# Transposes in one-chunk steps, a group's last banks emptied at once, seven products in K pairs 4 and 5, and a rough scale of the input, in an fp32 decoder layer

## The chip, the cores and the metric

One core of a Trainium2 chip runs the whole layer as one launch. The metric is the device time of that launch in microseconds: the median of several runs.

## What is computed

A decoder layer on 256 rows of width 2048, in fp32 (cut from the reference; the attention and the convolution are described below, since the change doesn't touch them):

```python
def swiglu(h, w_gate, w_up, w_down):
    return (jax.nn.silu(h @ w_gate) * (h @ w_up)) @ w_down

x = x + 0.5 * swiglu(rms_norm(x, ffn1_norm[l]), ffn1_w_gate[l], ffn1_w_up[l], ffn1_w_down[l])
x = x + hybrid_mixer(rms_norm(x, mix_norm[l]), w_in[l], b_gate[l], conv_w[l], ...)
x = x + 0.5 * swiglu(rms_norm(x, ffn2_norm[l]), ffn2_w_gate[l], ffn2_w_up[l], ffn2_w_down[l])
return rms_norm(x, final_norm)
```

The inner width of the two FFNs is 5632. `hybrid_mixer` is a combined projection into q, k, v, three convolution inputs and two gates, attention over 16 heads of 128, a short convolution, and three projections back.

## The kernel before, in words

**Products.** Every fp32 operand is kept as two parts: `hi`, rounded to the fp32r type, and `lo`, the rest. A product of a tile of 128x128 activations with 128x512 weights is three matmul pieces: hi by hi, hi by lo, lo by hi (L230 to L232). The weights come in tiles of 128x1024 fp32 (512 KB, called a chunk here: two K tiles of 512 columns), by SP's DMA queue (L793) into five buffers `w`. ScalarE makes `hi` (L824), VectorE `lo` = w - hi (L825). Four buffers each of `hi` and `lo` stand ready, so the split of a chunk waits until TensorE has finished the chunk four before it.

**Groups.** An FFN is a list of groups (`group`): gate and up groups over 1024 columns each (`gu`), and down groups (`down`). A group sums over 8 pairs of K tiles (16 tiles of 128 rows of the weights) into four PSUM banks `C[i, n]` (i: rows 0 to 127 or 128 to 255; n: left or right 512 columns). A plain pair is two chunks of 12 pieces. In a pair of the list `FAST` a seven-product scheme is used for the 2x2 block product: instead of 8 products 7, with sums of weight tiles, which VectorE makes (L797, four additions of 128x512 in `usum`), and sums of activation tiles, made when these are turned (`sums`). Such a pair has four chunks, of 6, 3, 6 and 6 pieces ("a", "b", "s1", "s2"), and its own four banks M[1], M[5], M[6], M[7], three of them (psS, psT, psV) those in which transposes are made too. Thirteen groups of each FFN have fast pairs; before they are pairs 1 and 3 (counted from 0).

**Order.** One program order is recorded by hand: `advance` puts the splits of chunks up to four ahead on ScalarE and VectorE, then TensorE's pieces of the chunk are recorded, then `flush(1)` records one piece of pending work: an entry of `pending` (emptying of banks), or else one of `turns` (transposes). While `banks_held`, from the first fast pair until all M banks are emptied, no turn is recorded. An engine runs its instructions in that order.

**Emptying.** `drain(C, n)` empties the two banks of n: after a gate group L497 combines them with the M sums and L471 applies silu into `gbuf`; after an up group L497 and L477 or L475 multiply `gbuf`. n = 0 is emptied in place; n = 1 is an entry of `pending`, recorded behind the next group's first chunk (`Step(chunks, pe, [lambda: drain(C, 1)])`).

**Turning.** The product of gate and up in `gbuf` is turned by transposes on TensorE (L309), two K tiles to a call of `turn_pair`, and split into `ring`. All of a `turn_pair` is recorded at once: transposes, copies (L102, L103, L315), sums (L296 to L301). The input of an FFN is turned in the same way (`turn_x`) into `xn`. For the second FFN its rows are scaled first by a rough scale, from the first quarter of the columns (L396, within the same call); the exact scale over the rough one is applied later. For the first FFN the exact scale of all of x is computed at the start, x is scaled (L878, L879) into `sacc`, and turned.

Of the kernel before, what the change touches and what calls it, by code (L numbers as in the profile page):

```python
# [14 lines left out]
P = 128  # L15
# [13 lines left out]
WARM = 11  # L29
FAST = (1, 3)  # L30
RING = 16
# [20 lines left out]
def macaron_kernel(ctx: ExitStack, tc: tile.TileContext, xt, gf, cst, wg1, wu1, wd1, win, wv, wao,  # L52
# [38 lines left out]

    work.tile([P, LINE + 112], F32, name="padw", tag="padw", bufs=1)

# [33 lines left out]
    def norm_cols(tag, i0=0, i1=2, blocks=NB):  # L127

        n = i1 - i0
        r = work.tile([P, 8], F32, name="rc", tag="rc", bufs=4)  # L130
# [82 lines left out]
    def group(wa, wb, k0, pairs, src, fast, xsum, early, drain):  # L213
# [77 lines left out]
    def sums(slot, a1, a2):  # L291
# [6 lines left out]
        nc.vector.tensor_add(x3, a2[:, 0:P], x6)  # L298
        nc.vector.tensor_sub(x7, a1[:, 0:P], a1[:, P:T])
        nc.scalar.copy(at[:, slot, :], c4)  # L300
        nc.vector.tensor_sub(at[:, slot + 1, :], c4, f32(at[:, slot, :]))  # L301

    def turn_pair(src, dst, gain, slot):

        keep = []
        for q, tag in ((0, "psT"), (1, "psV")):
            ps = patt.tile([P, 4 * P], F32, name=tag, tag=tag)
            for i in range(2):
                nc.tensor.transpose(ps[:, i * P:(i + 1) * P], src(q, i), ident)  # L309
            if slot is None:  # L310
                split_col(dst(q), ps[:, 0:T], None if gain is None else gain(q))
            else:
                a = tmp("a")
                if gain is None:
                    nc.scalar.copy(a, ps[:, 0:T])  # L315
                else:
                    nc.scalar.activation(a, ps[:, 0:T], AF.Copy, scale=gain(q))
                split_col(dst(q), a)
                keep.append(a)
        if keep:  # L320
            sums(slot, *keep)

    def turn_x(m, src, goff):

        slot = X_SUMS + 2 * FAST.index(m // 2) if m // 2 in FAST else None
        turn_pair(lambda q, i: src(m + q, i), lambda q: xn[:, m + q, :], lambda q: vec(goff, m + q), slot)

# [26 lines left out]

    def turn(m, gain):

# [6 lines left out]
    def residual(nb, factor, tag, gain):  # L363
# [16 lines left out]
        if tag == "f2":  # L380
            def done(pv):
                add(pv)
                if nb == 0:
                    scale0[0] = norm_cols(tag, blocks=1)
                if nb == NB - 1:
                    r = norm_cols(tag)
                    q = work.tile([P, 8], F32, name="rc", tag="rc", bufs=4)
                    nc.vector.reciprocal(q[:, 0:2], scale0[0])
                    nc.vector.tensor_mul(q[:, 2:4], r, q[:, 0:2])
                    rcol[tag] = q[:, 2:4]  # L390

                def scaled(m, i):
                    if i == 0:
                        t = pair[m] = tmp("xs")
                        for j in range(2):
                            nc.vector.tensor_scalar(t[:, j * P:(j + 1) * P], x[:, j, m * P:(m + 1) * P],  # L396
                                                    scale0[0][:, j:j + 1], None, op0=ALU.mult)
                    return pair[m][:, i * P:(i + 1) * P]
                pair = {}
                for m in (4 * nb, 4 * nb + 2):  # L400
                    turns.append(lambda m=m: turn_x(m, scaled, gain))
            return [done]
        if tag is None or tag == "fin":
            return [add]
        return [add, lambda _: None] + [lambda _, m=m: turn(m, gain) for m in range(4 * nb, 4 * nb + 4)]

# [11 lines left out]

    scale0 = [None]
    grow = {}  # L420
# [36 lines left out]

    def ffn(tag, wg, wu, wd, gain_next, next_tag, first=False):
        sign = {(0, 0): (0, ALU.add), (0, 1): (2, ALU.subtract), (1, 0): (3, ALU.add), (1, 1): (1, ALU.subtract)}
# [9 lines left out]
        def gate(i, src, cols):  # L469
            s = 1.0 if first else rcol[tag][:, i:i + 1]  # L470
            nc.scalar.activation(gbuf[:, i, cols], src, AF.Silu, scale=s)  # L471

        def up(i, src, cols):
            if first:
                nc.vector.tensor_mul(gbuf[:, i, cols], src, gbuf[:, i, cols])  # L475
            else:
                nc.vector.scalar_tensor_tensor(gbuf[:, i, cols], src, rcol[tag][:, i:i + 1], gbuf[:, i, cols],  # L477
                                               op0=ALU.mult, op1=ALU.mult)

        def hidden(q, t):  # L480

            k0 = next(a for a, b in ROUNDS if a <= t < b)
            p = (t - k0) // 2
            slot = H_SUMS + 2 * FAST.index(p) if p in FAST and k0 != ROUNDS[-1][0] else None
            turn_pair(lambda e, i: gbuf[:, i, (2 * q + e) * P:(2 * q + e + 1) * P],
                      lambda e: ring((t + e) % RING), None, slot)

        def gu(which, b):
            fast = () if (which, b) == ("g", 0) else FAST
            use = gate if which == "g" else up  # L490

            def drain(C, n):
                for i in range(2):
                    src = C[i, n]
# [4 lines left out]
                    use(i, src, slice(n * NW, (n + 1) * NW))  # L499
                if which == "u" and n == 1:  # L500
                    for q in range(4):
                        turns.append(lambda q=q: hidden(q, 8 * b + 2 * q))
            w = wg if which == "g" else wu
# [3 lines left out]
        def gu_last(n_block):  # L507
            def drain(C, n):
                for i in range(2):
                    (gate, up)[n](i, C[i, n], slice(0, NW))  # L510
                if n == 1:
                    for q in range(2):
                        turns.append(lambda q=q: hidden(q, 4 * n_block + 2 * q))
            steps.append(group(wg[n_block], wu[n_block], 0, ND // 2, lambda k: xn[:, k, :], (), None, None, drain))
# [256 lines left out]

    ffn("f1", wg1, wu1, wd1, GM, "mix", first=True)
    mixer(G2, "f2")
# [80 lines left out]
    nc.scalar.preload_act_table(AF.Sqrt)  # L854
    nc.sync.dma_start(cs[:, 0:NCST], cst)
    for nb in range(NB):
        cols = slice(nb * NW, (nb + 1) * NW)
        nc.sync.dma_start(x[:, :, cols], xt[:, :, cols])
    load(4)
    nc.vector.memset(gbuf[:, 0, 0:T], 0.0)  # L860
    warm = patt.tile([P, 4 * P], F32, name="psS", tag="psS")
    for _ in range(WARM):
        nc.tensor.matmul(warm[:, 0:T], gbuf[:, 0, 0:P], gbuf[:, 0, 0:T], start=True, stop=True)
    make_identity(nc, ident)
    for q0, sl in ((0, slice(0, P)), (P, slice(P, 3 * P))):
# [4 lines left out]
                                fill=NEG, base=q0, channel_multiplier=1)  # L870
    for nb in range(NB):
        for i in range(2):
            row_square("f1", i, nb, at[:, 8 + i, :])
    r = norm_cols("f1")
    cut(1)
    for nb in range(NB):
        cols = slice(nb * NW, (nb + 1) * NW)
        nc.vector.tensor_scalar(yout[:, 0, cols], x[:, 0, cols], r[:, 0:1], None, op0=ALU.mult)  # L878
        nc.scalar.activation(yout[:, 1, cols], x[:, 1, cols], AF.Copy, scale=r[:, 1:2])  # L879
    turns = []  # L880
    scaled_in = lambda m, i: yout[:, i, m * P:(m + 1) * P]
    for m in range(0, ND, 2):
        turns.append(lambda m=m: turn_x(m, scaled_in, G1))
    turns.pop(0)()
    turns.pop(0)()

    done = 0

    holding = False
    pending = []  # L890

# [6 lines left out]
    def flush(n=None):  # L898
        while pending and not holding and n != 0:
            pending.pop(0)()  # L900
            n = None if n is None else n - 1
        while turns and not banks_held and n != 0:
            turns.pop(0)()
            n = None if n is None else n - 1

# [68 lines left out]
```

## Time and profile before

| | us |
|---|---|
| median of 3 runs | 2530.03 |
| lowest and highest | 2527.68, 2531.37 |
| the profiled execution | 2531.69 |
| its span, first to last instruction | 2529.6 |
| TensorE busy | 2471.9 |
| VectorE busy | 1773.1 |
| ScalarE busy | 1231.9 |

A busy time is the union of an engine's instructions; the pieces of TensorE overlap one another in the rows, so their rate is read from start to start. The granted clock of TensorE over the span is 0.989: short stretches run at 0.5 (1.2 GHz), the rest at full rate (2.4 GHz). The program holds 11955 matmul instructions before and after.

### The profile page before, as it was taken

How to read it: one execution, taken by the hardware profiler on the slowest of the kernel's cores; microseconds unless marked ns; L12 is line 12 of the kernel's file. 1: busy time of each engine (PE TensorE's matmuls, PEld its weight loads, DVE VectorE, ACT ScalarE, POOL GpSimd, SP SyncE). 2: the span in 40 equal slices, each digit the busy share in tenths (PEclk: the TensorE clock that was granted, in tenths of full speed). 3: DMA queues.
4: the chain of work that ended last, by engine and by line, in shares of the span. 5: the costliest groups of instructions: out<-in, count | busy, mean ns of one | idle time of the engine just before them, and what ended most of it. 6: DMA issues, size and time to landing. Idle time of an engine off the chain costs nothing.

```text
span 2529.6 us, 31828 instructions
## 1 busy us (share of the span) xinstructions
PE 2471.9 (98%) x12030; PEld 2076.4 (82%) x12030; DVE 1773.1 (70%) x2343; ACT 1231.9 (49%) x1632; POOL 1.9 (0%) x10
## 2 busy tenths in 40 slices
PE   8999999999999999999999999998999999999998
PEld 6878887888888888888888888876787888788887
DVE  5777877888557777655555666665487787778765
ACT  5554545454445444444444454444455554545444
POOL 0000000000000000000000000000000000000000
PEclk9999999999999999999999999999999999999999
DMA  6555665656656555555555555554555565565664
GB/s 208 184 181 186 195 204 161 209 180 215 186 156 211 184 197 191 192 187 189 183 177 173 175 167 191 192 176 141 159 188 185 173 212 182 181 202 183 211 192 155
DMA packets 130841, 468.76 MB, mean 185 GB/s; under 512 B 14464, under 2 KB 14720, under 8 KB 130688
## 3 DMA queue, kind: packets, MB, share of 16 engines
q1 hardware_dynamic: 130400, 466.22, 57.9%
q8 instruction: 94, 1.54, 0.2%
q14 instruction: 59, 0.48, 0.1%
q10 hardware_dynamic: 288, 0.52, 0.1%
HBM read 464.58 MB, written 2.10 MB: 184 GB/s over the span
## 4 chain that ended last, share of the span: by engine, by line
PE 93%; DVE 3%; ACT 2%; issue 1%; DMA 0%; SPq 0%; DVEq 0%; ACTq 0%
PE ps L165 20%; PE pv L230 15%; PE pv L231 14%; PE pv L232 14%; PE ps L166 10%; PE pv L193 3%; PE pv L194 3%; PE pv L192 3%; PE pv L662 1%; PE pv L661 1%; PE pv L663 1%; DVE lo L825 1%; ACT hi L824 1%; PE psV L231 1%; PE psT L309 1%
## 5 line engine op out<-in xcount | busy, mean ns | idle before, releaser
L825 DVE TENSOR_TENSOR lo<-w,hi 128x1024 fp32r<-128x1024 f32 (+2 forms) x883 | 1031.6, 1184 | 525.8 <-ACT hi L824 517.6
L824 ACT CAST hi<-w 128x1024 fp32r<-128x1024 f32 (+2 forms) x883 | 888.4, 1018 | 676.9 <-PE pv L232 382.8
L165 PE MATMUL ps<-xn,hi 128*128 128x512 f32 x1744 | 611.8, 394 | 0.0
L230 PE MATMUL pv<-hi,xn 128*128 128x512 f32 x1228 | 490.0, 399 | 18.9 <-DVE sacc L497 18.6
L166 PE MATMUL ps<-xn,lo 128*128 128x256 f32 x1744 | 487.5, 280 | 0.0
L231 PE MATMUL pv<-lo,xn 128*128 128x512 f32 x1228 | 483.9, 394 | 0.3 <-DVE lo L825 0.3
L232 PE MATMUL pv<-hi,xn 128*128 128x512 f32 x1228 | 483.7, 394 | 0.0
L165 PEld LDWEIGHTS ps<-xn,hi 128*128 128x128 f32 x1744 | 327.4, 188 | 71.6
L166 PEld LDWEIGHTS ps<-xn,lo 128*128 128x128 f32 x1744 | 327.4, 188 | 0.5
L230 PEld LDWEIGHTS pv<-hi,xn 128*128 128x128 f32 x1228 | 234.1, 191 | 70.2 <-DVE sacc L497 22.2
L232 PEld LDWEIGHTS pv<-hi,xn 128*128 128x128 f32 x1228 | 233.8, 190 | 50.2
L231 PEld LDWEIGHTS pv<-lo,xn 128*128 128x128 f32 x1228 | 234.3, 191 | 47.9 <-DVE lo L825 0.6
L824 ACT CAST hi<-sacc 128x1024 fp32r<-128x1024 f32 x104 | 109.4, 1052 | 162.7 <-PE pv L232 135.2
L230 PE MATMUL pv<-hi,ring 128*128 128x512 f32 x432 | 168.5, 390 | 1.7 <-DVE sacc L497 1.7
L232 PE MATMUL pv<-hi,ring 128*128 128x512 f32 x432 | 168.1, 389 | 0.0
L231 PE MATMUL pv<-lo,ring 128*128 128x512 f32 x432 | 168.1, 389 | 0.0
L825 DVE TENSOR_TENSOR lo<-sacc,hi 128x1024 fp32r<-128x1024 f32 x104 | 127.1, 1222 | 48.7 <-ACT hi L824 48.5
L192 PE MATMUL pv<-hi,ring 128*128 128x512 f32 x304 | 122.0, 401 | 0.0
L193 PE MATMUL pv<-lo,ring 128*128 128x512 f32 x304 | 120.3, 396 | 0.0
L194 PE MATMUL pv<-hi,ring 128*128 128x512 f32 x304 | 120.2, 396 | 0.0
L230 PEld LDWEIGHTS pv<-hi,ring 128*128 128x128 f32 x432 | 81.1, 188 | 20.1 <-DVE sacc L497 3.4
L232 PEld LDWEIGHTS pv<-hi,ring 128*128 128x128 f32 x432 | 81.1, 188 | 16.8
(196 smaller groups left out, 2562.6 us busy)
## 6 DMA issues: line engine op xcount, KB each, us to landing
w<-in_win SPq DMA_DIRECT2D x218, 512.0 KB, 4.2
w<-in_wu SPq DMA_DIRECT2D x176, 512.0 KB, 4.3
w<-in_wd SPq DMA_DIRECT2D x176, 512.0 KB, 4.1
w<-in_wg SPq DMA_DIRECT2D x175, 512.0 KB, 3.9
w<-in_wco SPq DMA_DIRECT2D x32, 512.0 KB, 3.8
w<-in_wv SPq DMA_DIRECT2D x32, 512.0 KB, 4.3
w<-in_wao SPq DMA_DIRECT2D x32, 512.0 KB, 4.4
w<-in_wo SPq DMA_DIRECT2D x32, 512.0 KB, 4.0
```

Source lines behind the costliest of these rows:

```text
L165: nc.tensor.matmul(ps, hi[:, j * P:(j + 1) * P], r, start=(k == 0), stop=False)
L166: nc.tensor.matmul(ps[:, 0:T], lo[:, j * P:(j + 1) * P], r[:, 0:T], start=False, stop=(k == n - 1))
L192: nc.tensor.matmul(pv, xh, hi[:, cols], start=start, stop=False)
L193: nc.tensor.matmul(pv, xh, lo[:, cols], start=False, stop=False)
L194: nc.tensor.matmul(pv, xl, hi[:, cols], start=False, stop=stop)
L230: nc.tensor.matmul(ps, xh, hi[:, sl], start=start, stop=False)
L231: nc.tensor.matmul(ps, xh, lo[:, sl], start=False, stop=False)
L232: nc.tensor.matmul(ps, xl, hi[:, sl], start=False, stop=stop)
L309: nc.tensor.transpose(ps[:, i * P:(i + 1) * P], src(q, i), ident)
L661: nc.tensor.matmul(pv[i], xh, hi[:, cols], start=(k == 0), stop=False)
L824: nc.scalar.copy(hi[:, cols], w[:, cols])
L825: nc.vector.tensor_sub(lo[:, cols], w[:, cols], f32(hi[:, cols]))
```

## The change

1. **Turning in steps.** `turn` replaces `turn_pair`: a turned pair is a list of steps, S (scaling of x, only for an FFN's input), A (four transposes into one bank), B (copies and split), C and D (sums, where the pair is a fast one). `tick`, called once for each chunk from `flush`, records the next step of every turn in hand, at most one A to a chunk; a turn of `gbuf` begins two chunks late, and A comes two chunks behind S. The banks psS, psT and psV are used in rotation.
2. **Last banks.** At a group's end everything pending is recorded behind the last product of bank pair n = 0, then `drain(C, 0)`; `drain(C, 1)` follows directly behind the last product of n = 1.
3. **Fast pairs.** `FAST = (4, 5)`; the banks are held from pair 3 until the last pair.
4. **Rough scale in the first FFN too**, from the first quarter of x; the loads of the start are put in the order x quarter 0, weights 0 and 1, x 1, weights 2, x 2, weights 3, x 3, and cst goes by ScalarE's queue. The squares of the other quarters are pending work of the first group, and the exact scale over the rough one is made at that group's end.

```diff
-FAST = (1, 3)
+FAST = (4, 5)
...
                     if st:
-                        hold_banks(True)
+                        free_banks()
...
                     if sp:
                         pending.extend(early(M))
-                        pending.append(lambda: hold_banks(False))
...
-                    if last and n == 0:
-                        drain(C, 0)
+                    if fast and p == fast[0] - 1 and n == 0:
+                        hold_banks(True)
+                    if last:
+                        while pending:
+                            pending.pop(0)()
+                        if n == 0:
+                            hold_banks(False)
+                        drain(C, n)
...
-        return Step(chunks, pe, [lambda: drain(C, 1)], shift=0)
+        return Step(chunks, pe, [], shift=0)
...
+        def transposes():
+            tag = ("psS", "psT", "psV")[bank[0] % 3]
+            bank[0] += 1
+            ps = st["ps"] = patt.tile([P, 4 * P], F32, name=tag, tag=tag)
+            for q in range(2):
+                for i in range(2):
+                    nc.tensor.transpose(ps[:, (2 * q + i) * P:(2 * q + i + 1) * P], src(q, i), ident)
+            st["a"] = [ps[:, 0:T], ps[:, T:2 * T]]
...
+            if gains is None:
+                nc.scalar.copy(hi, both)
+                nc.vector.tensor_sub(lo, both, f32(hi))
+                if slot is not None:
+                    a = tmp("a")
+                    nc.scalar.copy(a, st["a"][0])
+                    st["a"][0] = a
+            elif slot is None:
+                for q in range(2):
+                    split_col(dst[:, q, :], st["a"][q], gains(q))
...
+    def tick():
+
+        taken = False
+        for t in list(turns):
+            if t[0] > 0:
+                t[0] -= 1
+                continue
+            if t[1][0][0] == "S" and sum(u[1][0][0] == "A" for u in turns) > 1:
+                continue
+            if t[1][0][0] == "A":
+                if taken or banks_held:
+                    taken = True
+                    continue
+                taken = True
+            step(t)
+            if not t[1]:
+                turns.remove(t)
...
+    load_x(0)
+    nc.scalar.dma_start(cs[:, 0:NCST], cst)
+    load(2)
+    load_x(1)
+    load(3)
+    load_x(2)
+    load(4)
+    load_x(3)
...
+    squares(0)
+    rough_scale("f1")
+    turns.extend(turn_x("f1", m, G1) for m in range(0, ND, 2))
...
         while pending and not holding and n != 0:
             pending.pop(0)()
             n = None if n is None else n - 1
-        while turns and not banks_held and n != 0:
-            turns.pop(0)()
-            n = None if n is None else n - 1
+        tick()
```

How the change moves VectorE's instructions in the second group of the first FFN (the first with fast pairs). `lo<-w,hi 128x1024` is a chunk's split, `sacc<-w` and `sacc<-sacc,w` are the additions for a fast pair (in `usum`, which lies in sacc), `lo<-sacc` the splits of chunks s1 and s2. Before:

```order
L825 TENSOR_TENSOR lo<-w,hi 128x1024 x10
L797 TENSOR_TENSOR sacc<-w 128x512 x2
L825 TENSOR_TENSOR lo<-w,hi 128x512
L797 TENSOR_TENSOR sacc<-sacc,w 128x512 x2
L825 TENSOR_TENSOR lo<-sacc,hi 128x1024 x2
L825 TENSOR_TENSOR lo<-w,hi 128x1024 x3
L797 TENSOR_TENSOR sacc<-w 128x512 x2
L825 TENSOR_TENSOR lo<-w,hi 128x512
L797 TENSOR_TENSOR sacc<-sacc,w 128x512 x2
L825 TENSOR_TENSOR lo<-sacc,hi 128x1024 x2
L825 TENSOR_TENSOR lo<-w,hi 128x1024 x4
```

After:

```order
L908 TENSOR_TENSOR lo<-w,hi 128x1024 x7
L880 TENSOR_TENSOR sacc<-w 128x512 x2
L908 TENSOR_TENSOR lo<-w,hi 128x512
L880 TENSOR_TENSOR sacc<-sacc,w 128x512 x2
L908 TENSOR_TENSOR lo<-sacc,hi 128x1024 x2
L908 TENSOR_TENSOR lo<-w,hi 128x1024
L880 TENSOR_TENSOR sacc<-w 128x512 x2
L908 TENSOR_TENSOR lo<-w,hi 128x512
L880 TENSOR_TENSOR sacc<-sacc,w 128x512 x2
L908 TENSOR_TENSOR lo<-sacc,hi 128x1024 x2
L908 TENSOR_TENSOR lo<-w,hi 128x1024 x4
```

Between the two fast pairs stood two plain chunks' splits and the next pair's chunk "a"; now the next pair's chunk "a" alone stands there.

VectorE at the end of the third group (gate), and the beginning of the fourth. L497 before and L580 after are the emptyings of a gate group's C banks, `ring` and `c` are turned pairs. Before:

```order
L825 TENSOR_TENSOR lo<-w,hi 128x1024
L497 TENSOR_TENSOR sacc<-pv,sacc 128x512 x2
L103 TENSOR_TENSOR ring<-a,ring 128x256 x2
L296 TENSOR_TENSOR c_1261<-a 128x128
L297 SCALAR_TENSOR_TENSOR c_1261<-c_1261,a 128x128
L298 TENSOR_TENSOR c_1261<-a,c_1261 128x128
L299 TENSOR_TENSOR c_1261<-a 128x128
L301 TENSOR_TENSOR at<-c_1261,at 128x512
L825 TENSOR_TENSOR lo<-w,hi 128x1024
L797 TENSOR_TENSOR sacc<-w 128x512 x2
L825 TENSOR_TENSOR lo<-w,hi 128x512
L497 TENSOR_TENSOR sacc<-pv,sacc 128x512 x2
```

After:

```order
L908 TENSOR_TENSOR lo<-w,hi 128x1024
L546 TENSOR_TENSOR sacc<-psS,sacc 128x512
L580 TENSOR_TENSOR sacc<-pv,sacc 128x512 x2
L908 TENSOR_TENSOR lo<-w,hi 128x1024
L580 TENSOR_TENSOR sacc<-pv,sacc 128x512 x2
L908 TENSOR_TENSOR lo<-w,hi 128x1024 x6
```

The second emptying stood behind a turned pair with its sums, a split, and the additions of a fast pair; now one split stands between the two emptyings.

VectorE in the last part of the mixer, behind the first quarter of the second FFN's input (L370 and L464 add to x). `xs` and, after, `gbuf` hold the scaled input. Before:

```order
L138 TENSOR_SCALAR rc<-rc 128x2
L139 TENSOR_TENSOR rc<-rc 128x2
L825 TENSOR_TENSOR lo<-w,hi 128x1024
L396 TENSOR_SCALAR xs<-x,rc 128x128 x2
L106 SCALAR_TENSOR_TENSOR xn<-psT,cs,xn 128x256
L396 TENSOR_SCALAR xs<-x,rc 128x128 x2
L106 SCALAR_TENSOR_TENSOR xn<-psV,cs,xn 128x256
L825 TENSOR_TENSOR lo<-w,hi 128x1024
L396 TENSOR_SCALAR xs<-x,rc 128x128 x2
L103 TENSOR_TENSOR xn<-a,xn 128x256
L396 TENSOR_SCALAR xs<-x,rc 128x128 x2
L103 TENSOR_TENSOR xn<-a,xn 128x256
```

After:

```order
L464 TENSOR_TENSOR x<-pv,x 128x512 x2
L407 TENSOR_SCALAR rc<-ssq 128x2
L409 RECIPROCAL rc<-rc 128x2
L398 TENSOR_SCALAR gbuf<-x,rc 128x256 x4
L908 TENSOR_TENSOR lo<-w,hi 128x1024 x3
L106 SCALAR_TENSOR_TENSOR xn<-psS,cs,xn 128x256 x2
L908 TENSOR_TENSOR lo<-w,hi 128x1024
L106 SCALAR_TENSOR_TENSOR xn<-psT,cs,xn 128x256 x2
```

The scalings stood between the readings of the transposes that wait for them and that TensorE ran in the same chunk; now all four stand together, three splits ahead of the first reading.

## Rows read from the trace of the kernel before

**Rows 1.** The page, busy time of each engine (share of span) x instructions.
```profile
PE 2471.9 (98%) x12030; PEld 2076.4 (82%) x12030; DVE 1773.1 (70%) x2343; ACT 1231.9 (49%) x1632; POOL 1.9 (0%) x10
```
**Rows 2.** List of waits of TensorE: us in total, times, longest.
```profile
PE pv L230 <- DVE sacc L497: 20.3, 8, 4.7
PE psV L309 <- DVE xs L396: 11.6, 8, 1.7
...
PE psT L309 <- DVE xs L396: 6.7, 5, 2.0
```
**Rows 3.** Stretches: length, busy us (count) by engine, granted clock, DMA share, GB/s.
```profile
68.75:110.91 42.16, 42.16 (x188) 34.91 (x186) 32.27 (x37) 21.36 (x23) 0.00 (x0) 1.00 0.62 200
150.00:172.00 22.00, 17.25 (x64) 13.28 (x63) 15.60 (x25) 11.54 (x19) 0.00 (x0) 0.84 0.31 96
250.00:257.00 7.00, 6.62 (x29) 5.18 (x28) 6.39 (x9) 3.65 (x6) 0.00 (x0) 1.00 0.12 22
...
1694.00:1806.00 112.00, 93.29 (x382) 73.69 (x381) 59.72 (x111) 45.29 (x70) 0.00 (x0) 0.92 0.45 137
1916.00:1938.00 22.00, 17.17 (x71) 13.38 (x70) 16.08 (x26) 12.82 (x20) 0.00 (x0) 0.92 0.31 96
...
2182.00:2204.00 22.00, 17.15 (x67) 13.28 (x66) 15.91 (x25) 12.46 (x20) 0.00 (x0) 0.84 0.30 96
```
**Rows 4.** Timeline of TensorE over a fast pair: start, us, what.
```profile
84.39 0.39 PE L230 MATMUL pv<-hi,xn 128*128 128x512 f32 x1
84.62 0.39 PE L231 MATMUL pv<-lo,xn 128*128 128x512 f32 x1
...
89.15 0.39 PE L230 MATMUL pv<-hi,xn 128*128 128x512 f32 x1
```
**Rows 5.** Timeline of VectorE up to and through that pair.
```profile
76.88 3.50 DVE L825 TENSOR_TENSOR lo<-w,hi 128x1024 fp32r<-128x1024 f32 x3
80.29 1.29 DVE L797 TENSOR_TENSOR sacc<-w 128x512 f32<-128x512 f32 x2
...
82.10 1.42 DVE L797 TENSOR_TENSOR sacc<-sacc,w 128x512 f32<-128x512 f32 x2
83.43 1.22 DVE L825 TENSOR_TENSOR lo<-sacc,hi 128x1024 fp32r<-128x1024 f32 x1
...
87.08 2.36 DVE L825 TENSOR_TENSOR lo<-w,hi 128x1024 fp32r<-128x1024 f32 x2
```
**Rows 6.** Timeline of ScalarE there (idle before, and who ended it).
```profile
85.99 2.01 ACT L824 CAST hi<-w 128x1024 fp32r<-128x1024 f32 x2 [0.31 <-PE pv L232]
```
**Rows 7.** Groups of VectorE by line: count, busy us, mean ns, idle before.
```profile
L797 DVE TENSOR_TENSOR sacc<-w 128x512 f32<-128x512 f32 x104 | 67.0, 686 | 0.0
```
**Rows 8.** Timeline at the end of the third group.
```profile
163.14 1.28 DVE L497 TENSOR_TENSOR sacc<-pv,sacc 128x512 f32<-128x512 f32 x2
...
163.88 0.79 PE L230 MATMUL pv<-hi,xn 128*128 128x512 f32 x1 [4.59 <-DVE sacc L497]
```
**Rows 9.** Timeline at the second FFN's first turned pair.
```profile
1700.87 0.47 DVE L396 TENSOR_SCALAR xs<-x,rc 128x128 f32<-128x128 f32 x2
1701.20 0.52 PE L309 MATMUL psT<-ident,xs 128*128 128x128 f32 x2 [1.96 <-DVE xs L396]
...
1703.00 0.69 PE L309 MATMUL psV<-ident,xs 128*128 128x128 f32 x2 [1.28 <-DVE xs L396]
```
**Rows 10.** Timeline of the start.
```profile
6.35 0.63 ACT L124 ACTIVATE at<-x 128x512 fp32r<-128x512 f32 x1 [4.34 <-DMA x<-in_xt]
...
11.37 0.63 ACT L124 ACTIVATE at<-x 128x512 fp32r<-128x512 f32 x1 [0.98 <-DMA x<-in_xt]
...
17.21 0.47 ACT L105 ACTIVATE xn<-psV,cs 128x256 fp32r<-128x256 f32 x1
17.32 0.48 DVE L106 SCALAR_TENSOR_TENSOR xn<-psT,cs,xn 128x256 fp32r<-128x256 f32 x1 [0.19 <-ACT xn L105]
...
18.62 0.78 PE L230 MATMUL pv<-hi,xn 128*128 128x512 f32 x1
```

More of the change, by code (lines that the diff above doesn't have):

```diff
@@ L299, in sums, with split_sums @@
         nc.vector.tensor_sub(x7, a1[:, 0:P], a1[:, P:T])
+        return c4
+    def split_sums(slot, c4):
         nc.scalar.copy(at[:, slot, :], c4)
         nc.vector.tensor_sub(at[:, slot + 1, :], c4, f32(at[:, slot, :]))
[L303 to L307, printed above, removed]
-            for i in range(2):
[L309 to L321, printed above, removed]
@@ L323, in turn_x, with turn, split, add @@
-    def turn_x(m, src, goff):
-        slot = X_SUMS + 2 * FAST.index(m // 2) if m // 2 in FAST else None
-        turn_pair(lambda q, i: src(m + q, i), lambda q: xn[:, m + q, :], lambda q: vec(goff, m + q), slot)
+    turns, bank = [], [0]
+    def turn(src, dst, gains, slot, delay=0, scale=None, spare=None):
+        st = {}
+        def transposes():
[6 more added lines that the diff above has]
+            st["a"] = [ps[:, 0:T], ps[:, T:2 * T]]
+        def split():
+            hi, lo = dst[:, :, 0:T], dst[:, :, T:2 * T]
+            both = st["ps"].rearrange("p (a b) -> p a b", b=T)
+            if gains is None:
[8 more added lines that the diff above has]
+                    split_col(dst[:, q, :], st["a"][q], gains(q))
+            else:
+                a = spare()
+                for q in range(2):
+                    nc.scalar.activation(a[:, q * T:(q + 1) * T], st["a"][q], AF.Copy, scale=gains(q))
+                st["a"] = [a[:, 0:T], a[:, T:2 * T]]
+                a2 = a.rearrange("p (a b) -> p a b", b=T)
+                nc.scalar.copy(hi, a2)
+                nc.vector.tensor_sub(lo, a2, f32(hi))
+        def add():
+            st["c4"] = sums(slot, *st["a"])
+        t = []
+        if scale is not None:
+            t.append(("S", scale, 1))
+        t += [("A", transposes, 0), ("B", split, 0)]
+        if slot is not None:
+            t += [("C", add, 0), ("D", lambda: split_sums(slot, st["c4"]), 0)]
+        return [delay, t]
@@ new lines, in step @@
+    def step(t):
+        _, fn, wait = t[1].pop(0)
+        fn()
+        t[0] = wait
+    def tick():
[14 more added lines that the diff above has]
+                turns.remove(t)
@@ new lines, in free_banks, with turn_x, scale @@
+    def free_banks():
+        for t in list(turns):
+            while t[1] and t[1][0][0] in "BC":
+                step(t)
+            if not t[1]:
+                turns.remove(t)
+    xs_at = [gbuf[:, i, j * NW:(j + 1) * NW] for i in range(2) for j in range(2)]
+    def turn_x(tag, m, goff):
+        xs = xs_at[m // 2 % 2].rearrange("p (a b) -> p a b", b=T)
+        def scale():
+            for i in range(2):
+                nc.vector.tensor_scalar(xs[:, i, :], x[:, i, m * P:(m + 2) * P], scale0[tag][:, i:i + 1], None,
+                                        op0=ALU.mult)
+        slot = X_SUMS + 2 * FAST.index(m // 2) if m // 2 in FAST else None
+        return turn(lambda q, i: xs[:, i, q * P:(q + 1) * P], xn[:, m:m + 2, :], lambda q: vec(goff, m + q), slot,
+                    scale=scale, spare=lambda: xs_at[2 + m // 2 % 2])
@@ L328, in last_job @@
+    scale0 = {}
     def last_job(chunks, src, post):
@@ L383, in done @@
                 if nb == 0:
-                    scale0[0] = norm_cols(tag, blocks=1)
+                    rough_scale(tag)
                 if nb == NB - 1:
[L386 to L401, printed above, removed]
+                    exact_over_rough(tag)
+                turns.extend(turn_x(tag, m, gain) for m in (4 * nb, 4 * nb + 2))
             return [done]
@@ L404, in residual @@
             return [add]
-        return [add, lambda _: None] + [lambda _, m=m: turn(m, gain) for m in range(4 * nb, 4 * nb + 4)]
+        return [add, lambda _: None] + [lambda _, m=m: turn_one(m, gain) for m in range(4 * nb, 4 * nb + 4)]
     def finish(i):
@@ L469, in gate @@
         def gate(i, src, cols):
-            s = 1.0 if first else rcol[tag][:, i:i + 1]
-            nc.scalar.activation(gbuf[:, i, cols], src, AF.Silu, scale=s)
+            nc.scalar.activation(gbuf[:, i, cols], src, AF.Silu, scale=rcol[tag][:, i:i + 1])
         def up(i, src, cols):
[L474 to L478, printed above, removed]
+            nc.vector.scalar_tensor_tensor(gbuf[:, i, cols], src, rcol[tag][:, i:i + 1], gbuf[:, i, cols],
+                                           op0=ALU.mult, op1=ALU.mult)
         def hidden(q, t):
@@ L492, in drain @@
             def drain(C, n):
+                assert which == "u" or not any(t[1][0][0] in "SA" for t in turns)
+                if which == "g" and b == 0 and n == 0:
+                    exact_over_rough_once(tag)
                 for i in range(2):
@@ L499, in drain @@
                     use(i, src, slice(n * NW, (n + 1) * NW))
-                if which == "u" and n == 1:
-                    for q in range(4):
-                        turns.append(lambda q=q: hidden(q, 8 * b + 2 * q))
+                if which == "u":
+                    for q in (2 * n, 2 * n + 1):
+                        hidden(q, 8 * b + 2 * q)
             w = wg if which == "g" else wu
@@ L770, in mixer @@
             steps.append(wide_job(wide(wo, nb), ring, residual(nb, None, next_tag, gain_next)))
-    ffn("f1", wg1, wu1, wd1, GM, "mix", first=True)
+    ffn("f1", wg1, wu1, wd1, GM, "mix")
     mixer(G2, "f2")
@@ L870, in macaron_kernel, with squares @@
                                 fill=NEG, base=q0, channel_multiplier=1)
-    for nb in range(NB):
+    def squares(nb):
         for i in range(2):
             row_square("f1", i, nb, at[:, 8 + i, :])
-    r = norm_cols("f1")
+    squares(0)
+    rough_scale("f1")
+    turns.extend(turn_x("f1", m, G1) for m in range(0, ND, 2))
     cut(1)
[L876 to L883, printed above, removed]
-    turns.pop(0)()
-    turns.pop(0)()
     done = 0
     holding = False
-    pending = []
+    pending = [lambda nb=nb: squares(nb) for nb in range(1, NB)]
     banks_held = False
@@ L901, in flush @@
             n = None if n is None else n - 1
-        while turns and not banks_held and n != 0:
-            turns.pop(0)()
-            n = None if n is None else n - 1
+        tick()
+    for t in turns[0:2]:
+        step(t)
+    for t in turns[0:2]:
+        step(t)
+        step(t)
+    del turns[0:2]
+    tick()
+    tick()
     for s in steps:
```

38 lines of the change are left out of this document (26 added, 12 removed).

## The prediction

> **What bounds the kernel now.** I read the page first: TensorE is busy for 2471.9 of 2529.6 us [rows 1]. Only two things can change the time: the pieces that TensorE runs, and the times at which it stands or runs at half clock. The change leaves the number of products alone (two fast pairs in a group before and after, 52 in all: a fast pair makes four additions of 128x512, two of each form, and [rows 7], one of two such forms, counts 104; the transposes stay too). So I read the list of waits next: TensorE waits 20.3 us for the emptying of the C banks (L497), 11.6 and 6.7 us for the scaled input of the second FFN (L396) [rows 2], and a stretch at the start. Then the stretches around these waits, because behind a wait the clock falls as well. In a quiet stretch 188 pieces take 42.16 us, 0.224 each with the few missing records; piece to piece the timeline has 0.227 us (84.39 to 84.62) [rows 3, 4]. What a stretch holds beyond its count x 0.227 is lost.
>
> **What the change removes.**
>
> 1. The last emptying of a group. At 158.9 TensorE stands 4.59 us for L497, which VectorE begins at 163.14, behind a turned pair's sums, a weight split and two additions [rows 8]. The stretch 150 to 172 holds 64 pieces, 4 of them transposes (0.36 us together): 60 x 0.227 + 0.36 = 14.0 of 22 us, so 8.0 lost, and the granted clock of 0.84 says that part of it is a fall to half clock (1.2 GHz) behind the wait [rows 3]. The same stands there four times: 416 to 438, a copy of this stretch, 1916 to 1938 with 71 pieces (6.4 lost) and 2182 to 2204 with 67 (7.4 lost). Together **30 us**. After the change the emptying stands on VectorE directly behind the last product of its bank, ahead of the next split, and the turns of the group before are long done. Is anything late next? Emptying two banks of an up group is four operations of about 0.7 (two take 1.28 in the row), 2.7 us; the next group needs the first of these banks one chunk (12 x 0.227 = 2.72 us) later, and the first is free after 0.7, the second after 2.0. The splits behind them have a lead: four chunks are in flight and a split ends 2.6 us after its buffer is free (3.92 less 1.36, below), so it ends 3 x 2.72 - 2.6 = 5.6 us before its product. I take all 30; bounds 24 and 30.
> 2. Four short waits of the same kind where `down` begins: 250 to 257 holds 29 pieces, 6.6 of 7 us [rows 3]; 0.4 to 0.6 each, **2 us**.
> 3. The second FFN's input. Now the scaling (L396) and its transposes are recorded together, so TensorE reaches the transpose while VectorE still splits: 1.96 us of waiting, then 1.28 more for the second half [rows 9]; so it goes for all eight pairs. 1694 to 1806 holds 382 pieces, 32 of them transposes: 350 x 0.227 + 2.9 = 82.4 of 112 us, 29.6 lost at a clock of 0.92 [rows 3]. The change scales two chunks (5.4 us) ahead and transposes later; Four scalings, of which two short ones take 0.47 now [rows 9], fit into that. Some 2 us remain (the first banks of the next group still wait for the squares): **28 us**; bounds 20 and 29.
> 4. The start. Now all four quarters of x are squared before anything is scaled: the squares of the first begin at 6.35, those of the last at 11.37, and the first product comes at 18.62, 7.25 us behind them [rows 10]. In the change the same path (squares, scale, split of the first weights, scaling, transposes, copies) hangs on the first quarter alone and begins 11.37 - 6.35 = 5.0 us earlier; it is also shorter, without the second half of the scale's computation and with 2 of 16 column blocks to scale, by some 2 to 3 us. The weights that now come between the quarters of x are no loss, since they are wanted as early. Before its first products TensorE is hardly busy, so I expect a stretch at half clock as now, which then falls on products: some of it comes back. **7 us**; bounds 3 and 10.
>
> In that path the rows show two banks in use side by side: ScalarE reads psV from 17.21 for 0.47 while VectorE reads psT from 17.32 for 0.48 [rows 10]. The change puts both halves of a pair in one bank. The Trainium skill, page "PSUM — Partial Sum Buffer", section "PSUM bank collisions raise a hardware error", asks that no two engines touch the same bank and partitions at the same time, which would make the four readings a chain. By that rule the readings of a pair take 4 x 0.48 = 1.9 us instead of 1.4 and those of the two first pairs 1 us more, so the start gains 6 us; by the rows alone it gains 7. No run here shows one bank read by both at once.
>
> Sum removed: 30 + 2 + 28 + 7 = **67 us**.
>
> **What the change adds.** Two fast pairs in succession. TensorE runs a fast pair in 4.76 us, 21 pieces, 84.39 to 89.15 [rows 4]; VectorE needs for it three whole splits (1.14 apart: three in 3.50), one half split and four additions, 6.5 us. Now a normal pair (5.44 us of TensorE, two splits, 2.3 us of VectorE) lies between two fast ones, and VectorE recovers; in the change fast pair 4 is followed by fast pair 5. How far does it fall behind? Count from TensorE's start on pair 4, t = 0 (84.39 in the row of a fast pair). A split can't begin before the hi buffer of four chunks earlier is free. So the first split of the pair behind gets its hi part at 1.60 and its lo part at 2.69 (85.99 and 87.08 less 84.39), done at 3.92 [rows 5, 6]. VectorE's order from that lo part to the third chunk's lo part is, today, third of three splits at 79.16 (76.88 + 2 x 1.14), two additions at 80.29, half split, two additions at 82.10, split from 83.43 to 84.65: 5.49 us without a pause [rows 5]. The same order stands in the change for pair 5, so the lo part of its third chunk is there at 2.69 + 5.49 = 8.18. TensorE wants it with the second piece of that chunk: pair 4, then the chunks of 6 and of 3 pieces and one piece, 4.76 + 1.36 + 0.68 + 0.23 = 7.03. It waits 8.18 + 0.06 - 7.03 = **1.2 us**. The hand-off of 0.06 is that of an emptying: the first of the two from 163.14 has its 0.68 over at 163.82, and the piece goes at 163.88 [rows 8]. The fourth chunk's lo part comes at about 9.4 and is wanted at 9.6, so it adds nothing. 26 groups have such pairs: 26 x 1.2 = **31 us**. No row shows two fast pairs in succession. Bounds: 0 if VectorE gets at the additions of pair 5 earlier than its order says; 1.7 if the fourth chunk or a weight transfer waits too. I take the chain, since every link has its row. No DMA is added but the order: cst moves to ScalarE's queue, the weights go in between quarters of x. Both are in the start's term.
>
> The cover goes for nothing else: transposes and turns now end by the fifth pair, where VectorE has no other work.
>
> **Sum.** The profiled execution took 2531.7 us. 2531.7 - 67 + 31 = 2495.7. The median of the runs shown is 1.7 below it: **2494 us**. Own range of this case, with the bounds of its terms (26 x 0.9 to 1.7; removed 60 to 70): 2482 to 2514.
>
> **The rivals.**
>
> *The fast pairs cost nothing* (0.13). If a split leads by more than I count, the 31 us don't come: 2494 - 31 = 2463. For it: outside the fast pairs each split leads by 5.6 us. Against it: the lead is tied to four buffers, and four short chunks hold half as much of TensorE's time.
>
> *The turned pairs still hold TensorE* (0.13). The change would then not do what it says in the x turns: a chain of scaling, copy and split that VectorE runs behind its own queue lets half of the 28 + 7 us stay. 2494 + 17.5 = 2511. For it: the start's first turns run before any product covers them. Against it: two chunks lie between scaling and transpose.
>
> *Each new wait drops the clock* (0.12, the case on the other side). The place is the third chunk of pair 5. A wait of 4.59 us is followed by a granted clock of 0.84 in its 22 us stretch [rows 8, 3]: 0.16 x 22 = 3.5 us of work lost, 7 us at half clock. If 1.2 us in a dense stretch were enough for half of that, each group would lose 1.7 more: 26 x 1.7 = 44, 2494 + 44 = 2538. The point from which it decides is 67 / 26 = 2.6 us for a group; over that the change is slower. Against it: the stretch from 250 to 257 waits too and keeps a clock of 1.00, while the fallen stretches held waits two to four times as long [rows 3, 9].
>
> **Chances.** The forecast 0.62, the rivals 0.13, 0.13 and 0.12. From 2463 to 2522 lie the first three and the milder part of the last. About 0.2% (5 us) is what a measurement of this kernel can tell from no change. Faster by more than that: the first three, 0.88. The last gives 0.09 for slower and 0.03 for the same.
>
> **What would show it.** In the profile after: no wait for the emptying of a bank (now L580) over 1 us; nothing on the scaled input; first product before 13 us; the granted clock at 1.00 in the stretches where it was 0.84 and 0.92; and 26 waits of about 1.2 us of L231 for a lo part (L908), each in the third chunk of pair 5, with the clock at full rate through them. I am wrong if these waits are missing or over 2 us, or if half-clock stretches follow them.

## The result, and the profile after

The changed kernel takes **2493.24 us** (median of 4 runs, 2493.06 to 2493.31), the kernel before 2530.7 beside it: ratio 0.9853, 95% interval 0.9836 to 0.987. Forecast were 2494 us. The sum came out right; its terms did less well, and one of its reasons was wrong.

The list of waits of TensorE after the change (us in total, times, longest), to be read against [rows 2]:

```profile
PE psS L231 <- DVE lo L908: 27.6, 26, 1.3
PE psS L323 <- DVE gbuf L398: 1.3, 1, 1.3
PE psS L954 <- DVE gbuf L951: 1.2, 1, 1.2
PE pv L231 <- DVE lo L908: 0.9, 1, 0.9
PE pv L230 <- ACT pv L124: 0.4, 1, 0.4
```

The waits for emptied banks and for the scaled input of the second FFN are gone. One new line stands at the top, with exactly 26 entries: the lo part of a split. Here it is in the timeline of the second group, through the first three chunks' splits of pair 5 (start, us, what):

```profile
83.11 1.23 DVE L908 TENSOR_TENSOR lo<-sacc,hi 128x1024 fp32r<-128x1024 f32 x1 [1.50 <-ACT hi L907]
...
84.47 1.23 DVE L908 TENSOR_TENSOR lo<-w,hi 128x1024 fp32r<-128x1024 f32 x1
...
85.61 1.29 DVE L880 TENSOR_TENSOR sacc<-w 128x512 f32<-128x512 f32 x2
...
86.82 0.68 DVE L908 TENSOR_TENSOR lo<-w,hi 128x512 fp32r<-128x512 f32 x1
...
87.42 1.41 DVE L880 TENSOR_TENSOR sacc<-sacc,w 128x512 f32<-128x512 f32 x2
...
88.58 0.39 PE L230 MATMUL psS<-hi,at 128*128 128x512 f32 x1
88.75 2.50 DVE L908 TENSOR_TENSOR lo<-sacc,hi 128x1024 fp32r<-128x1024 f32 x2
...
90.02 0.50 PE L231 MATMUL psS<-lo,at 128*128 128x512 f32 x1 [1.05 <-DVE lo L908]
...
90.36 0.40 PE L232 MATMUL psS<-hi,at 128*128 128x512 f32 x1
```

VectorE runs without a pause from 84.47 to 89.97 (88.75 and one split of 1.22): 5.50 us, the chain of 5.49 that was read from [rows 5]. TensorE's second piece could start at 88.81 and starts at 90.02, 1.21 us late. The "1.05" of the row counts from the modelled end of the piece before; start to start is the measure.

The stretches (length, busy us and count by engine, granted clock, DMA share, GB/s) that answer to [rows 3]:

```profile
9.00:31.00 22.00, 19.92 (x96) 15.58 (x97) 18.60 (x38) 17.74 (x35) 0.00 (x0) 1.00 0.83 285
84.00:96.00 12.00, 10.95 (x48) 8.71 (x48) 11.78 (x14) 7.74 (x10) 0.00 (x0) 1.00 0.45 148
140.00:162.00 22.00, 22.00 (x99) 18.22 (x98) 15.24 (x18) 10.76 (x12) 0.00 (x0) 1.00 0.71 239
1664.00:1776.00 112.00, 111.64 (x508) 92.07 (x507) 70.73 (x103) 55.89 (x81) 0.00 (x0) 1.00 0.63 188
```

The end of the third group (140 to 162) is full of products where [rows 3] had 64 pieces in 22 us. The last part of the mixer holds 508 pieces in 112 us in place of 382. The clock is at 1.00 in all four, behind the new waits too (84 to 96).

**Where the time went, by stage.** Equal pieces of work are found in both traces by their first products: of the second group, the mixer, the mixer's last projection and the second FFN's second group. Before, then after:

```profile
68.75 0.39 PE L230 MATMUL pv<-hi,xn 128*128 128x512 f32 x1
...
758.04 0.48 PE L446 MATMUL ps<-xn,hi 128*128 128x512 f32 x1
...
1671.85 0.40 PE L192 MATMUL pv<-hi,ring 128*128 128x512 f32 x1
...
1835.48 0.39 PE L230 MATMUL pv<-hi,xn 128*128 128x512 f32 x1
```

```profile
59.61 0.39 PE L230 MATMUL pv<-hi,xn 128*128 128x512 f32 x1
...
748.30 0.48 PE L525 MATMUL ps<-xn,hi 128*128 128x512 f32 x1
...
1662.12 0.40 PE L192 MATMUL pv<-hi,ring 128*128 128x512 f32 x1
...
1797.27 0.39 PE L230 MATMUL pv<-hi,xn 128*128 128x512 f32 x1
```

| stage | before | after | difference |
|---|---|---|---|
| start and first group | 68.75 | 59.61 | -9.1 |
| rest of the first FFN | 689.3 | 688.7 | -0.6 |
| mixer | 913.8 | 913.8 | 0.0 |
| last projection, first group of the second FFN | 163.6 | 135.2 | -28.5 |
| rest, to the end of the span (2529.6, 2491.5) | 694.1 | 694.2 | +0.1 |

The whole gain lies in two stages. In the thirteen groups of each FFN that have fast pairs, what was removed and what was added cancel: 0.6 us in one FFN, nothing in the other. That is the point to look at next.

### The profile page after: what moved, and what is told of

Read it like the earlier page. It is cut to its first block, busy times and chain, and to the rows that moved or that the text cites. A ratio compares the mean times of both kernels' runs of the same rounds, so it can differ in the third digit from the quotient of the medians.

```text
span 2491.5 us, 31739 instructions
## 1 busy us (share of the span) xinstructions
PE 2451.4 (98%) x12030; PEld 2063.2 (83%) x12030; DVE 1763.4 (71%) x2290; ACT 1216.7 (49%) x1573; POOL 1.9 (0%) x10
## 4 chain that ended last, share of the span: by engine, by line
PE 92%; DVE 5%; ACT 1%; issue 1%; DMA 0%; ACTq 0%; DVEq 0%
PE ps L165 21%; PE pv L232 14%; PE pv L230 14%; PE pv L231 14%; PE ps L166 11%; PE pv L194 3%; PE pv L192 3%; PE pv L193 3%; DVE sacc L880 3%; DVE lo L908 2%; ACT hi L907 1%; PE pv L744 1%; PE pv L745 1%; PE pv L746 1%; PE psS L231 1%
## 5 line engine op out<-in xcount | busy, mean ns | idle before, releaser
L230 PE MATMUL pv<-hi,xn 128*128 128x512 f32 x1228 | 483.2, 394 | 0.5 <-ACT pv L124 0.4
L231 PE MATMUL pv<-lo,xn 128*128 128x512 f32 x1228 | 478.6, 390 | 0.9 <-DVE lo L908 0.9
L232 PE MATMUL pv<-hi,xn 128*128 128x512 f32 x1228 | 479.0, 390 | 0.0
L232 PEld LDWEIGHTS pv<-hi,xn 128*128 128x128 f32 x1228 | 230.6, 188 | 48.7 <-DVE xn L106 0.2
L230 PEld LDWEIGHTS pv<-hi,xn 128*128 128x128 f32 x1228 | 230.7, 188 | 48.1 <-ACT pv L124 0.8
L231 PEld LDWEIGHTS pv<-lo,xn 128*128 128x128 f32 x1228 | 230.8, 188 | 47.9 <-DVE lo L908 1.2
L230 PE MATMUL pv<-hi,ring 128*128 128x512 f32 x432 | 168.2, 389 | 0.0
L231 PE MATMUL pv<-lo,ring 128*128 128x512 f32 x432 | 168.2, 389 | 0.0
L231 PEld LDWEIGHTS pv<-lo,ring 128*128 128x128 f32 x432 | 81.1, 188 | 16.9
L230 PEld LDWEIGHTS pv<-hi,ring 128*128 128x128 f32 x432 | 81.1, 188 | 16.9
```

The costliest lines, as they stand in the source:

```text
L230: nc.tensor.matmul(ps, xh, hi[:, sl], start=start, stop=False)
L231: nc.tensor.matmul(ps, xh, lo[:, sl], start=False, stop=False)
L232: nc.tensor.matmul(ps, xl, hi[:, sl], start=False, stop=stop)
```

## The experiments

**1. A plain pair between the fast pairs.** The changed kernel with one line altered:

```diff
-FAST = (4, 5)
+FAST = (3, 5)
```

> The changed kernel with the fast pairs at 3 and 5, a plain pair between them. Theory (VectorE falls behind in two fast pairs in succession): the 26 waits of 1.2 us of L231 for a lo part vanish, because a plain pair gives VectorE 5.44 us of TensorE's time for two splits (2.3 us); 2493 - 31 = 2462 us, at most 5 more if the turned pairs of the group before now reach into the first fast pair. Rival (the waits belong to these banks or to a late weight transfer, wherever the fast pairs stand): the waits stay at 1.2 us each, time within 5 us of 2493.

Measured: **2457.12 us** (2457.08 to 2457.63), ratio to the kernel before 0.9711 (0.9694 to 0.9727). The list of waits has no line for L231 in a fast group any more; what is left of it:

```profile
PE psS L323 <- DVE gbuf L398: 1.5, 1, 1.5
PE psS L954 <- DVE gbuf L951: 1.2, 1, 1.2
PE pv L231 <- DVE lo L908: 0.9, 1, 0.9
PE pv L230 <- ACT pv L124: 0.4, 1, 0.4
```

The 26 waits belong to the succession of the two pairs. They cost 2493.2 - 2457.1 = 36 us, 1.39 each and not 1.2. The rest is in the rows of the changed kernel above: the piece behind the wait follows 0.34 us after it (90.02 to 90.36) instead of 0.23, and the pieces behind that one lose another 0.05 us together. By the stages of the table, both traces are alike but for the groups with fast pairs: 17.8 us in the first FFN and 18.2 in the second.

**2. The chain shortened, the pairs left where they are.** The additions of pair 5 go ahead of pair 4's last split:

```diff
             elif kind == "s2":
+                if chunks[c + 1][4] == "a":
+                    load(c + 3)
+                    first_sums(raw[c + 1], raw[c + 2])
+                    added.add(c + 2)
                 w = usum[:, 2 * NW:4 * NW]
```

(`first_sums` holds the two additions of chunk "b", which are left out there when they were `added`.)

> The fast pairs stay at 4 and 5; alone the first two additions of pair 5 are recorded ahead of the last split of pair 4, where VectorE stands idle for about 1.5 us until a buffer comes free. Theory (the chain of VectorE's instructions is what comes late, not its total work): the chain of 5.49 us loses the 1.2 us of two additions, the lo part of the third chunk is there at 6.96 where 7.03 is wanted, so each of the 26 waits falls from 1.2 us to 0.0 to 0.1 and the time to 2462 to 2465 us. Rival (VectorE's total work in the two pairs, 13 us for 9.5 us of TensorE, is the limit): moving it inside the pairs changes little, the wait comes in another chunk, 2485 to 2493 us.

Measured: 2462.86 us (2462.83 to 2463.19), ratio 0.9733 (0.9718 to 0.9747). VectorE in the second group:

```profile
82.00 1.29 DVE L880 TENSOR_TENSOR sacc<-w 128x512 f32<-128x512 f32 x2
83.46 1.23 DVE L917 TENSOR_TENSOR lo<-sacc,hi 128x1024 fp32r<-128x1024 f32 x1 [0.17 <-ACT hi L916]
84.82 1.82 DVE L917 TENSOR_TENSOR lo<-w,hi 128x1024 fp32r<-128x1024 f32 x2
86.57 1.41 DVE L880 TENSOR_TENSOR sacc<-sacc,w 128x512 f32<-128x512 f32 x2
87.90 2.50 DVE L917 TENSOR_TENSOR lo<-sacc,hi 128x1024 fp32r<-128x1024 f32 x2
```

The two additions now fill the pause of 1.50 us that stood before 83.11 in the changed kernel, and the list of waits has no line for the lo part of a fast pair any more. So it was the order of VectorE's instructions, not its amount of work: the same instructions, 30 us less. Experiment 1 is 5.7 us faster still, 0.2 us for a group; about half of that stands at the same place, where the piece behind still follows 0.34 us later:

```profile
89.17 0.50 PE L231 MATMUL psS<-lo,at 128*128 128x512 f32 x1
89.51 0.39 PE L232 MATMUL psS<-hi,at 128*128 128x512 f32 x1
```

**3. The chain made longer.** The second two additions of pair 5 are made twice:

```diff
-                add(usum[:, 2 * NW:3 * NW], usum[:, 0:NW], b[:, NW:2 * NW])
-                add(usum[:, 3 * NW:4 * NW], usum[:, 2 * NW:3 * NW], a[:, NW:2 * NW])
+                for _ in range(2 if c >= 4 and chunks[c - 4][4] == "s1" else 1):
+                    add(usum[:, 2 * NW:3 * NW], usum[:, 0:NW], b[:, NW:2 * NW])
+                    add(usum[:, 3 * NW:4 * NW], usum[:, 2 * NW:3 * NW], a[:, NW:2 * NW])
```

> The changed kernel with the two additions of the third chunk of pair 5 done twice (the result stays the same). Theory: the chain grows by 0.61 + 0.72 = 1.3 us and each of 26 waits from 1.2 to 2.5 us: 2493 + 34 = 2527 us with the clock at full rate through the waits. Rival (a wait of this length in a dense stretch lowers the clock): half-clock stretches behind the waits, 1.7 us more for each, 2571 us if behind all. If VectorE had slack there, neither: under 2500 us.

Measured: 2550.49 us (2547.8 to 2551.37), ratio 1.0077 (1.0062 to 1.0092), slower than the kernel before. Neither theory has it alone. The waits, and two stretches around them:

```profile
PE psS L231 <- DVE lo L909: 65.3, 26, 2.8
```

```profile
88.00:100.00 12.00, 9.49 (x35) 7.31 (x34) 10.72 (x13) 6.51 (x8) 0.00 (x0) 0.86 0.68 216
183.00:195.00 12.00, 9.49 (x42) 7.54 (x41) 11.81 (x14) 6.69 (x9) 0.00 (x0) 1.00 0.66 217
```

Each wait grew from 1.06 to 2.51 us (65.3 and 27.6 over 26), 1.45 x 26 = 38 us. Behind the first wait the clock fell, with 35 pieces in 12 us; behind the third, of the same length in the same place of a group, it did not, with 42. In the trace 13 of the 26 waits have a half-clock stretch behind them. A stretch like the first loses 0.14 x 12 = 1.7 us, 13 of them 22. 38 + 22 = 60, measured 57. The rival of the prediction on the slower side is real, then. By the list of waits it begins, for single waits in a dense stretch, between 1.7 us (0 of the 4 that experiment 6 has) and 2.5 us (13 of 26); at 1.06 us it is 0 of 26.

**4. The second emptying put back.** `drain(C, 1)` returns to the pending work of the next group:

```diff
-                        drain(C, n)
+                        if n == 0:
+                            drain(C, 0)
...
-        return Step(chunks, pe, [], shift=0)
+        return Step(chunks, pe, [lambda: drain(C, 1)], shift=0)
```

> The changed kernel with the second emptying of a group put back behind the next group's first chunk and its split, all else as changed. Theory by which the emptying in place removed the four waits of 4.6 us: these come back at the ends of four groups, with their half clock, 2493 + 25 to 30 = 2518 to 2523 us. Rival by which it was the turned pairs, finished now before the fast pairs and no longer in front of the emptying: only waits of 0.4 to 0.6 us come back, at up to 26 group ends, so 2494 to 2508 us and no fall of the clock.

Measured: 2501.91 us (2501.61 to 2502.02), ratio 0.9887 (0.9872 to 0.9901): 8.7 us more than the changed kernel. New in the list of waits:

```profile
PE pv L230 <- DVE x L601: 2.8, 8, 0.4
```

Eight short waits at and behind down groups, and no wait of 4.6. Piece by piece the two traces part at the beginnings of 16 groups: 0.62 us at the eight with such a wait, 0.34 us at eight others, 7.7 us together. In the changed kernel, with its fast pairs at 4 and 5, emptying the last banks at once is worth 9 us, not 30.

**5 and 6. The kernel before with the fast pairs moved, and nothing else.** `FAST = (4, 5)` in experiment 5, `FAST = (3, 5)` in experiment 6. In both, the fourth quarter of a gate or up group is combined with a sum that the first emptying has already overwritten (the change's emptying of everything pending first is what prevents this); the instructions, their sizes and their order are those of the kernel otherwise. What stands too late for a right result is one addition of 0.69 us in a group.

> The kernel before with the fast pairs at 4 and 5 and nothing else changed. Theory (the four waits of 4.6 us came from turned pairs that stood in front of the emptying, because the banks were held from pair 1 on; with the fast pairs late these are turned early): the four waits and their half clock go, 30 us, and the 26 waits for a lo part come, 26 x 1.37 = 36 us with the small rest in the next chunk: 2530 - 30 + 36 = 2536 us. Rival (the turning in steps or the emptying in place was needed): the four waits stay, 2566 us.

> The kernel before with the fast pairs at 3 and 5 and nothing else changed. Theory: the four waits go and no wait for a lo part comes: 2530 - 30 = 2500 us, with the waits on the scaled input, the start and the short waits at the first banks of the down groups left as before. Rival (steps or emptying in place needed): 2525 to 2532 us.

Measured: 2545.91 us (2545.74 to 2545.99, ratio 1.0063, 1.0048 to 1.0078) and 2504.27 us (2501.73 to 2505.89, ratio 0.9898, 0.9883 to 0.9913). The waits with (4, 5), then with (3, 5):

```profile
PE psS L231 <- DVE lo L825: 27.3, 26, 1.1
...
PE psT L309 <- DVE ring L103: 6.1, 4, 1.5
PE pv L230 <- DVE x L517: 2.9, 8, 0.4
```

```profile
...
PE psS L231 <- DVE lo L825: 6.9, 4, 1.7
...
```

The line "pv L230 <- DVE sacc L497: 20.3" is missing from both. So the place of the fast pairs alone removed the four long waits: with the banks held from a later pair, the turned pairs of the group before are finished earlier and no longer stand in front of an emptying. At (4, 5) the move alone is a loss, 16 us, since its own 26 waits cost more than it removes. Of the 10 us over the expectation some 7 lie in the FFNs' groups, where the last two rows of the first list stand, and 2 in the start. At (3, 5) four waits of 1.7 are left, in which a whole turned pair with its sums is recorded in front of a fast pair's additions; experiment 1, with the same place and turning in steps, has none of them. They and what follows them are 8 of the 11 us by which the FFNs' groups are longer than in experiment 1. That is what the steps do in the groups. At (3, 5) no short wait for an emptied bank is in the list, so emptying late costs at most the other 3 us there.

**7. The scaling of x in the step of its transposes.**

```diff
-        t = []
-        if scale is not None:
-            t.append(("S", scale, 1))
-        t += [("A", transposes, 0), ("B", split, 0)]
+        def scale_and_transpose():
+            if scale is not None:
+                scale()
+            transposes()
+
+        t = [("A", scale_and_transpose, 0), ("B", split, 0)]
...
     for t in turns[0:2]:
         step(t)
-        step(t)
```

> The changed kernel with the scaling of x recorded in the same step as its transposes, not two chunks ahead; all else as changed. Theory (the lead of the scaling is what removed the waits on the scaled input): TensorE waits again, now once for a pair's four transposes in place of twice: 6 to 8 pairs x 1.6 to 2.0 us and some half clock behind them, 2493 + 10 to 20 = 2503 to 2513 us. Rival (the rotation of three banks and the single emptying did it): under 2497 us.

Measured: 2519.08 us (2518.55 to 2520.51), ratio 0.9957 (0.9943 to 0.9971): 26 us more than the changed kernel, over the expected 10 to 20. The expectation had counted the second FFN's turns and forgotten those of the start. Two stretches, and the start's TensorE:

```profile
9.00:31.00 22.00, 13.83 (x57) 10.53 (x58) 14.92 (x32) 14.78 (x31) 0.00 (x0) 0.77 0.67 240
1690.00:1800.00 110.00, 99.77 (x435) 80.45 (x434) 60.97 (x92) 50.16 (x72) 0.00 (x0) 0.97 0.55 159
...
14.42 1.16 PE L323 MATMUL psV<-ident,gbuf 128*128 128x128 f32 x4 [3.26 <-DVE gbuf L400]
18.05 1.08 PE L323 MATMUL psS<-ident,gbuf 128*128 128x128 f32 x4 [2.46 <-DVE gbuf L400]
18.78 0.78 PE L230 MATMUL pv<-hi,xn 128*128 128x512 f32 x1
...
71.15 0.39 PE L230 MATMUL pv<-hi,xn 128*128 128x512 f32 x1
```

From 9 to 31 it runs 57 pieces where the changed kernel runs 96, with part of them at half clock. The third and fourth pair's scaling and transposes now stand ahead of the first product, which comes at 18.78 and not at 11.30, and the second group begins at 71.15 and not at 59.61: 11.5 us. The stage from the last projection to the second FFN's second group takes 149.65 us where the changed kernel takes 135.15 and the kernel before 163.63. So the lead is worth 14.5 of the 28.5 us gained there, about half. The other half stays without it; whether the four transposes of a pair in one step (one wait where there were two) or the three banks in turn bring it was not tried.

**8. Three fast pairs where no turned pairs wait.** From experiment 1's variant, with `FAST, MORE = (3, 5), (1, 3, 5)`: up and down groups use `MORE`, gate groups `FAST`.

> The variant with fast pairs at 3 and 5 (2457 us), with a third one, pair 1, in the nine groups of each FFN in front of which no turned pairs are waiting (up and down groups). Theory (a plain pair between two fast ones is enough for VectorE, however many there are): 18 groups lose 3 pieces of 0.227 us each, 2457 - 12 = 2445 us, without waits for a lo part. Rival (pair 1 meets the emptying of the group before, as in the kernel before): waits for banks or lo parts of 0.5 us and more in these groups take the gain, 2455 us and over.

Measured: **2448.48 us** (2447.0 to 2449.69), ratio 0.9678 (0.9664 to 0.9692), the fastest version here, though 3 us over the expectation. No wait for a lo part is left in its fast groups. The lost part is at the start:

```profile
9.00:31.00 22.00, 18.56 (x76) 13.94 (x76) 17.45 (x37) 14.84 (x30) 0.00 (x0) 0.84 0.76 261
...
64.08 0.39 PE L230 MATMUL pv<-hi,xn 128*128 128x512 f32 x1
```

The second group begins at 64.08 and not at 59.43 as in experiment 1: the sums for pair 1 are now made between the first turned pairs, and the clock falls there (0.84). 12.3 us gained in 18 groups less about 4.6 at the start leaves 8 of the 12.

## Why the prediction was right, and where it was not

- **Two fast pairs in succession, +31 us.** Right in place, mechanism and count; 25 waits of 1.21 us start to start and one of 1.49, forecast 1.2. Experiment 2 shows that the chain sets it: without the wait 30 us go. The term itself was 36 us by experiment 1: what follows a wait, mostly the next piece's 0.11 us, had been put at nothing.
- **The group ends, -30 and -2 us.** The rest of both FFNs came out at -0.6 and 0.1 us, with 36 added, so 36 were removed; 4 more than the sum had. But the step "the emptying stands on VectorE directly behind the last product of its bank" was given as the reason, with the earlier turns beside it. By experiments 4 to 6 the move of the fast pairs removes the four long waits alone, and emptying at once is worth 9 us. In other words the move of the pairs, which the prediction entered as a cost only, removes by itself most of what its 26 waits cost: in experiment 5 the FFNs' groups take 12.6 us more than in the kernel before, with some 36 us of such waits among them, so some 23 were removed.
- **The second FFN's input, -28 us.** 28.5. The reason given, the scaling two chunks ahead, accounts for 14.5 of them by experiment 7; the cause of the rest is open.
- **The start, -7 us.** 9.1, within its bounds: the first product comes at 11.30 (forecast before 13), 7.3 us earlier, and the half-clock stretch that was expected on the first products did not come. In experiments 7 and 8 it did, behind waits of 1.3 us and more among the first turned pairs, and in experiments 2 and 3 for seven or eight pieces: there TensorE reaches the first transposes 2.6 and 2.8 us after the last of the matmuls on zeros that open the program, here and in experiment 1 after 1.7 and 1.9. In those two it cost next to nothing, since the second group begins at 59.95 and 59.58. Which of the start's edits, the rough scale or the order of the loads, brought the 9.1 was not tried.
- **One bank for both halves.** The rows of the changed kernel have ScalarE waiting for VectorE between two readings of psS, and 2.02 us for a pair's four (the first product stands among them):

```profile
10.77 0.47 ACT L105 ACTIVATE xn<-psS,cs 128x256 fp32r<-128x256 f32 x1 [2.15 <-PE psS L323]
11.28 0.48 DVE L106 SCALAR_TENSOR_TENSOR xn<-psS,cs,xn 128x256 fp32r<-128x256 f32 x1 [0.62 <-ACT xn L105]
...
11.30 0.51 PE L230 MATMUL pv<-hi,xn 128*128 128x512 f32 x1
...
11.80 0.47 ACT L105 ACTIVATE xn<-psS,cs 128x256 fp32r<-128x256 f32 x1 [0.55 <-DVE xn L106]
...
12.31 0.48 DVE L106 SCALAR_TENSOR_TENSOR xn<-psS,cs,xn 128x256 fp32r<-128x256 f32 x1 [0.54 <-ACT xn L105]
```

  VectorE has to wait for ScalarE in any case, since `lo` is made from `hi`; that ScalarE waits for VectorE is new. That is the order which the section on bank collisions of the page "PSUM — Partial Sum Buffer" of the Trainium skill asks for, at 2.02 us where 1.9 had been worked out. What overlap in one bank would do was not tried.
- **The rivals.** "Each new wait drops the clock" did not come at 1.2 us, and experiment 3 shows it half come at 2.5. "The fast pairs cost nothing" is what experiments 1 and 2 make of the kernel: 2457 and 2463 us, forecast 2463. "The turned pairs still hold TensorE" did not come: the second FFN's input has no wait left.
- **The range.** Its lower end comes out at 2483 from the terms beside it, not 2482; and with the bounds that the terms themselves were given (49 to 71 us removed) it would have been wider.

The sum was right because two errors cancelled: about 7 us more were removed than forecast, and about 5 more added. That it lies within 1 us is luck.

## What to carry to other kernels

A wait of TensorE for VectorE need not mean that VectorE has too much to do: walk along its order from the last pause to the late result, and look whether something in that chain could have stood in the pause. A change that gains in one place and pays in another should be run in parts: here one line of it was worth 36 us of loss, and (3, 5) in place of (4, 5) gives them back. When several edits could have removed a wait, undo one at a time before naming the cause.

## What was not expected of the hardware

The length of a wait alone did not decide whether the granted clock fell. In one kernel (experiment 3) 26 waits at the same place of otherwise dense groups, 25 of them of one length, 2.67 us start to start (2.51 by the list of waits), were followed by a half-clock stretch 13 times and by none 13 times. 26 waits of 1.21 us (one of 1.49) never were, nor were the four of 1.88 us (1.7 by the list) of experiment 6; the four of 4.6 us of the kernel before were each time. What else told the 13 from the 13 was not found. A cost for a wait between these can only be given as a range: for 2.5 us of waiting it was 0 or 1.7 us on top.
